# Rotary quadrants by ScalarE copies, odd Fourier tiles in the unit ring, and large elementwise operations moved from GpSimd to VectorE in a two-layer diffusion trunk

## The chip, the cores and the metric

The kernel runs on one core of a Trainium2 chip. A core has a tensor engine for matrix products (PE, with the loading of weights, PEld, shown apart), a vector engine (VectorE, DVE), a scalar engine (ScalarE, ACT), GpSimd (POOL), and SyncE (SP), whose queue here issues nearly all transfers from HBM. Each engine works through its own instructions in order and waits on semaphores for the others. The metric is the device time of one execution in microseconds; less is better.

## The reference

Two streams of 256 tokens (latent and context, width 1024) go through two layers. Each layer normalises and modulates its input, projects it by `w_in`, runs three branches, gates and merges them, and ends with a SwiGLU block. In the last layer only the latent stream is carried on. What matters here is the rotation of the queries and keys of the attention branch (latent tokens only), and the Fourier branch:

```python
def _rope(x, cos, sin):
    x1, x2 = jnp.split(x, 2, axis=-1)
    return jnp.concatenate([x1 * c - x2 * s, x1 * s + x2 * c], axis=-1)

def _fourier(u):
    z = u.astype(jnp.float32).reshape(B, T, FN_GROUPS, FN_GC)      # 4 groups of 256 channels
    y = jnp.fft.fftn(z, axes=(1, 3), norm='ortho').real
    return y.reshape(B, T, FN_W).astype(u.dtype)
```

The attention's head halves are 32 wide, so that in a layout with channels on the 128 partitions the two halves `x1` and `x2` of a head lie in neighbouring quadrants of 32 partitions. The modulation that opens a layer (a product of the conditioning vector with `w_ada`) has to be known before the first projection.

## The kernel before

**Precision.** Products of full precision are made from parts: a weight tile is loaded as float32 (`raw`), ACT rounds it to a high part (`split_hi`, L215), and the difference is the low part (`split`, L223 on POOL where `pool` is set, L225 on DVE elsewhere). Activations are held as a high and a low part too. Three products high x high, high x low and low x high are accumulated (L310 to L312 in `proj_t`).

**Jobs.** `prog` is a list of jobs, each with one weight tile of 512 KB. `run_all` goes through it: before job i runs, the tiles up to i + 4 are split and the loads up to i + 8 are issued (`upto`). The raw tiles, high parts and low parts have four buffers each. All other large tiles (activations, tables, results) are units of 4 KB a partition from a ring of 32 (`upool`, `unit()`). Transfers are issued from SP in the order in which the program names them, so one that waits for a buffer holds those behind it. Between jobs the program interleaves side work in small steps (`side`, `tick`).

**The opening.** The modulation of layer 0 is computed in four quarters (`AdaPart`: products L456, copy L461, transposing products L466, then `finish`, L470 to L472 on DVE). Each quarter lets two of the eight channel blocks of the activations be modulated (`h_banks`: L569 on ACT for the high part, L572 and L578 on DVE for the low part). `opening_jobs` runs the first four projection jobs quarter by quarter (L748), in an order written out by hand for PE, DVE, ACT and POOL (`begin`, `in_order`). In `mm(i, k, which)`, `which` 0 is high x high, 1 the low part of the weights, 2 the low part of the activations. Job 0's low part is made on POOL.

**Rotation.** Each key and query tile of 128 channels is projected into one PSUM bank of 512 columns, 256 context and 256 latent. L1476 copies the context columns by ACT. `rope` rotates the latent columns: four DVE products, one for each quadrant, that read the neighbouring quadrant of the PSUM bank and the sine table (L1317), one DVE product with the cosine table (L1318), and the sum on POOL (L1319). There are 16 such tiles a layer.

**Folding and Fourier tiles.** The transform over the tokens is split into even and odd parts. `fold_h` folds the activations while the queries are projected (the sum of high and low part at L829, on DVE for even i and on POOL for odd i; folds at L836 and L837; in layer 0 a new split at L844 and L845). `proj_z` then runs eight Fourier jobs, in pairs of an even and an odd tile of the weights (`FoldZ`). Both tiles of a pair are loaded into raw buffers. The split of a Fourier job folds the pair into a unit (L861: sum for the even one, difference for the odd one), and both splits read both raw tiles. In layer 0 (`do_split`, products L884 to L886) the folded tile is split again into parts; in layer 1 it goes to float32 products (L888), and there the odd folds are on POOL.

**Gate tile.** Behind the Fourier jobs comes `GateJob`, whose weight tile is cleared by POOL (L232), filled by four small transfers (L234) and split with its low part on POOL (L223).

Of the kernel before, what the change touches and what calls it, by code (L numbers as in the profile page):

```python
# [8 lines left out]
F32 = mybir.dt.float32  # L9
# [3 lines left out]
ALU = mybir.AluOpType  # L13
# [30 lines left out]
def tile_trunk(ctx: ExitStack, tc: tile.TileContext, x, c, cx, c_ctx, w_ada, b_ada, norm_g, w_in, ml_gate_b,  # L44
# [150 lines left out]
    class Job:  # L195

        pool = first = in_units = False
# [19 lines left out]
        def split(self):  # L217
            if not self.do_split:
                return
            self.split_hi()  # L220
            raw = self.raw
            if self.pool:
                G.tensor_tensor(out=self.lo, in0=raw, in1=self.hi.bitcast(F32), op=ALU.subtract)  # L223
            else:
                V.tensor_tensor(out=self.lo, in0=raw, in1=self.hi, op=ALU.subtract)  # L225

    class GateJob(Job):
        pool = True

# [503 lines left out]
    def opening_jobs(bd, specs, parts):  # L733
# [3 lines left out]
        def run(job):  # L737
# [11 lines left out]
            def hl(i, q):  # L749
                for k in (2 * q, 2 * q + 1):  # L750
                    mm(i, k, 2)
# [18 lines left out]
            hl(0, 0)  # L770
            for which in range(3):
                for k in range(2):
                    mm(1, k, which)
# [30 lines left out]
        for i, (cls, src, _) in enumerate(specs):  # L804
            prog.append(cls(src, KB, 128, run))
            prog[-1].first = True

            prog[-1].pool = i == 0

# [5 lines left out]
    def fold_h(h, ns, res, st):  # L815
# [8 lines left out]
        for k in range(0, KB, per):  # L824
            f = unit()
            fv = f.rearrange("p a n -> p (a n)").rearrange("p (k n) -> p k n", k=per)
            for i in range(k // 2, (k + per) // 2):
                sm = unit()[:, :, n0:]
                (G if i % 2 else V).tensor_tensor(out=sm, in0=h[0][i][:, :, n0:], in1=h[1][i][:, :, n0:], op=ALU.add)  # L829
# [20 lines left out]
    class FoldZ(Job):  # L850
# [3 lines left out]
        def load(self):  # L854
            super().load()
            self.tile = self.raw

        def split(self):
            a, b = (self.mate.tile, self.tile) if self.odd else (self.tile, self.mate.tile)
            self.raw = unit().rearrange("p a (b n) -> p (a b) n", b=4)  # L860
            (G if self.odd and not self.do_split else V).tensor_tensor(out=self.raw[:, :, 1:128], in0=a[:, :, 1:128], in1=b[:, :, 127:0:-1],  # L861
                                               op=ALU.subtract if self.odd else ALU.add)
# [449 lines left out]
    def rope(ps, u):  # L1312

        r = tmp(256)
        for a in range(4):
            src = slice(32 * (a ^ 1), 32 * (a ^ 1) + 32)
            V.tensor_tensor(out=r[32 * a:32 * a + 32, :], in0=ps[src, 256:512], in1=ropes[src, :], op=ALU.mult)  # L1317
        V.tensor_tensor(out=u[:, 256:512], in0=ps[:, 256:512], in1=ropec, op=ALU.mult)  # L1318
        G.tensor_tensor(out=u[:, 256:512], in0=u[:, 256:512], in1=r, op=ALU.add)  # L1319
# [402 lines left out]
def make_consts():  # L1722
# [13 lines left out]
    k[:, C_RS:C_RS + 256] = np.tile(np.concatenate([np.sin(ang).T, -np.sin(ang).T]), (2, 1))  # L1736
# [37 lines left out]
```

## Time and profile before

| | |
|---|---|
| median of 3 runs | 1935.72 us (1934.77 to 1935.95) |
| the profiled execution's own time | 1936.41 us |
| its span in the profile | 1934.7 us |
| PE, DVE, ACT, POOL busy | 97%, 62%, 40%, 7% of the span |
| largest groups of POOL | L1319 42.0 us, L1338 23.0 us |
| mean HBM traffic | 140 GB/s over the span |

Times in the profile are microseconds from the start of the span. A row of the order of time gives start, duration, engine, line, operation, written tile `<-` read tiles, shape, and in brackets the idle time of the engine before it and what ended it. A row of a group gives the count, the total busy time in us, the mean of one in ns, and the idle time before. A row of the waits gives the total in us, how often, and the longest. PE's products overlap, so that a product's duration is longer than the distance to the next one. POOL's L1338 lies in the attention stage, behind the stages that are changed here.

### The profile page before, as it was taken

Reading aid. Unit: us, or ns where it says so; the run is one execution under the profiler, and the core shown is the slowest. Engines: PE = TensorE matmul, PEld = TensorE weight load, DVE = VectorE, ACT = ScalarE, POOL = GpSimd, SP = SyncE. Lnnn points to the kernel's source line nnn. Section 1 sums busy time; section 2 is a strip of 40 time slices with the busy share of each in tenths; the row PEclk is TensorE's granted clock in tenths of the full one; section 3 lists DMA queues with packets and bytes.
Section 4 is the critical chain, followed back from the end, with each engine's and each line's share of the span. In section 5 each row is a group of like instructions: output and inputs, shape, how many; then the busy total and the mean of one; then the engine's idle time right before and its main releaser. Section 6 shows DMA issues by size and latency. Waiting matters only on the chain. (4 is left out here: it accounts for less than half of the span.)

```text
span 1934.7 us, 27570 instructions
## 1 busy us (share of the span) xinstructions
PE 1885.0 (97%) x10428; PEld 1579.5 (82%) x10428; DVE 1201.4 (62%) x2626; ACT 782.5 (40%) x1470; POOL 144.8 (7%) x168
## 2 busy tenths in 40 slices
PE   7999999999999999999999999999999999999998
PEld 4778787888877888788777887887888889979996
DVE  5796688852467567653334235777985477666655
ACT  3333476632343333352222224323873354345442
POOL 0231100000001110000000000150100011000000
PEclk9999999999999999999999999999999999999999
DMA  9557522134322334534442333675322664676663
GB/s 311 183 163 211 177 66 66 55 91 128 109 66 71 100 99 122 194 96 138 127 141 88 120 98 110 186 204 190 99 67 77 186 194 123 180 240 178 183 197 129
DMA packets 339679, 268.99 MB, mean 139 GB/s; under 512 B 17181, under 2 KB 295933, under 8 KB 339546
## 3 DMA queue, kind: packets, MB, share of 16 engines
q1 hardware_dynamic: 338824, 264.60, 45.9%
q10 hardware_dynamic: 722, 2.62, 0.3%
q8 instruction: 82, 1.34, 0.3%
q14 instruction: 51, 0.42, 0.1%
HBM read 264.44 MB, written 6.91 MB: 140 GB/s over the span
## 5 line engine op out<-in xcount | busy, mean ns | idle before, releaser
L225 DVE TENSOR_TENSOR wl<-wr,wh 128x1024 fp32r<-128x1024 f32 x335 | 419.0, 1253 | 408.2 <-ACT wh L215 400.8
L215 ACT CAST wh<-wr 128x1024 fp32r<-128x1024 f32 x336 | 351.9, 1050 | 651.3 <-issue 234.4
L310 PE MATMUL m<-u,wh 128*128 128x512 f32 (+1 forms) x1736 | 608.0, 350 | 0.9 <-ACT wh L215 0.9
L312 PE MATMUL m<-u,wl 128*128 128x512 f32 (+1 forms) x1736 | 595.7, 343 | 2.3 <-DVE wl L225 2.3
L311 PE MATMUL m<-u,wh 128*128 128x512 f32 (+1 forms) x1736 | 594.7, 343 | 0.0
L310 PEld LDWEIGHTS m<-u,wh 128*128 128x128 f32 x1736 | 329.1, 190 | 47.9 <-issue 4.0
L312 PEld LDWEIGHTS m<-u,wl 128*128 128x128 f32 x1736 | 328.7, 189 | 42.4 <-DVE wl L225 3.6
L311 PEld LDWEIGHTS m<-u,wh 128*128 128x128 f32 x1736 | 329.2, 190 | 38.2 <-issue 3.1
L331 PE MATMUL m<-wh,u 128*128 128x512 f32 x532 | 214.9, 404 | 0.0
L333 PE MATMUL m<-wh,u 128*128 128x512 f32 x532 | 207.9, 391 | 0.0
L332 PE MATMUL m<-wl,u 128*128 128x512 f32 x532 | 207.9, 391 | 0.0
L331 PEld LDWEIGHTS m<-wh,u 128*128 128x128 f32 x532 | 100.0, 188 | 24.3 <-issue 4.5
L333 PEld LDWEIGHTS m<-wh,u 128*128 128x128 f32 x532 | 99.9, 188 | 21.0
L332 PEld LDWEIGHTS m<-wl,u 128*128 128x128 f32 x532 | 100.1, 188 | 20.5 <-issue 1.4
L1360 ACT ACTIVATE u<-p,s 128x512 f32<-128x512 f32 (+1 forms) x96 | 59.4, 618 | 39.3 <-DVE s L1359 37.2
L623 PE MATMUL m<-wh,u 128*128 128x512 f32 x180 | 70.3, 391 | 0.2 <-ACT wh L215 0.2
L624 PE MATMUL m<-wl,u 128*128 128x512 f32 x180 | 70.1, 390 | 0.0
L625 PE MATMUL m<-wh,u 128*128 128x512 f32 x180 | 69.9, 389 | 0.0
L1319 POOL TENSOR_TENSOR u<-u,t 128x256 f32<-128x256 f32 x32 | 42.0, 1312 | 304.1 <-DVE u L1318 254.5
L1626 DVE SCALAR_TENSOR_TENSOR t<-t,m 128x512 f32<-128x512 f32 (+1 forms) x44 | 24.4, 554 | 63.2 <-PE m L312 62.7
L1357 DVE TENSOR_REDUCE s<-p 128x1 f32<-128x512 f32 (+1 forms) x96 | 57.1, 595 | 6.6 <-PE p L1355 6.4
L1317 DVE TENSOR_TENSOR t<-m,ctab 32x256 f32<-32x256 f32 x120 | 50.5, 421 | 4.1 <-ACT u L1476 1.2
(308 smaller groups left out, 2518.6 us busy)
## 6 DMA issues: line engine op xcount, KB each, us to landing
wr<-in_w_in_dram SPq DMA_DIRECT2D x176, 512.0 KB
wr<-in_w_ffn_in_dram SPq DMA_DIRECT2D x88, 512.0 KB
u<-in_w_ada_dram SPq DMA_DIRECT2D x80, 512.0 KB
wr<-in_w_ffn_out_dram SPq DMA_DIRECT2D x44, 512.0 KB
u<-in_w_ada_dram SPq DMA_DIRECT2D x32, 256.0 KB
wr<-in_w_br_da_dram SPq DMA_DIRECT2D x16, 512.0 KB
wr<-in_w_br_ml_dram SPq DMA_DIRECT2D x16, 512.0 KB
wr<-in_w_out_dram SPq DMA_DIRECT2D x16, 512.0 KB
```

Of the source, the lines that this page charges most:

```text
L215: S.copy(self.hi, self.raw)
L225: V.tensor_tensor(out=self.lo, in0=raw, in1=self.hi, op=ALU.subtract)
L310: T.matmul(ps[:, n0:], lhsT=job.hi[:, k, :], rhs=ah, start=(k == 0), stop=False)
L311: T.matmul(ps[:, n0:], lhsT=job.hi[:, k, :], rhs=al, start=False, stop=False)
L312: T.matmul(ps[:, n0:], lhsT=job.lo[:, k, :], rhs=ah, start=False, stop=(k == KB - 1))
L331: T.matmul(st[tb], lhsT=ah, rhs=job.hi[:, j, :], start=(k == 0), stop=False)
L332: T.matmul(st[tb], lhsT=ah, rhs=job.lo[:, j, :], start=False, stop=False)
L333: T.matmul(st[tb], lhsT=al, rhs=job.hi[:, j, :], start=False, stop=(k == nk - 1))
L623: T.matmul(ps[tb], lhsT=ah, rhs=job.hi[:, j, :], start=(k == 0), stop=False)
L624: T.matmul(ps[tb], lhsT=ah, rhs=job.lo[:, j, :], start=False, stop=False)
L625: T.matmul(ps[tb], lhsT=al, rhs=job.hi[:, j, :], start=False, stop=(k == nk - 1))
L1360: S.activation(p[:, m, :nk], sp[:, :nk], AF.Exp, bias=nb, scale=0.125, accum_out=d[:, m:m + 1])
```

## The change

- **Opening:** job 0's low part is made on DVE, like all others. The first products of the opening are put in another order: behind job 0's products with the high part of the activations come job 1's with the high part of the weights, then both jobs' products with the low part of the activations, then job 1's with the low part of the weights.
- **Rotation:** ACT copies each quadrant of the latent columns from PSUM into its neighbour's place in an SBUF tile `r`, and DVE multiplies `r` with the sine table in one operation over 128 partitions and adds it. The sign of the sine table is exchanged, since it is now read at the place of the result.
- **Folding:** all sums of `fold_h` and all folds of `FoldZ` are on DVE.
- **Fourier tiles:** the odd tile of a pair is loaded into a unit of the ring, the even one into a raw buffer as before.
- **Gate tile:** its low part is made on DVE. POOL still clears it.

```diff
     class Job:
-        pool = first = in_units = False
+        first = in_units = False
...
             raw = self.raw
-            if self.pool:
-                G.tensor_tensor(out=self.lo, in0=raw, in1=self.hi.bitcast(F32), op=ALU.subtract)
-            else:
-                V.tensor_tensor(out=self.lo, in0=raw, in1=self.hi, op=ALU.subtract)
+            V.tensor_tensor(out=self.lo, in0=raw, in1=self.hi, op=ALU.subtract)
 
     class GateJob(Job):
-        pool = True
-
...
             h(0, 0)
-            hl(0, 0)
-            for which in range(3):
+            for i, which in ((1, 0), (0, 2), (1, 2), (1, 1)):
                 for k in range(2):
-                    mm(1, k, which)
+                    mm(i, k, which)
...
-            prog[-1].pool = i == 0
...
                 sm = unit()[:, :, n0:]
-                (G if i % 2 else V).tensor_tensor(out=sm, in0=h[0][i][:, :, n0:], in1=h[1][i][:, :, n0:], op=ALU.add)
+                V.tensor_tensor(out=sm, in0=h[0][i][:, :, n0:], in1=h[1][i][:, :, n0:], op=ALU.add)
...
         def load(self):
-            super().load()
+            if self.odd:
+
+                self.raw = unit().rearrange("p a (b n) -> p (a b) n", b=4)
+                nc.sync.dma_start(self.raw, self.src.rearrange("(k p) n -> p k n", p=128))
+            else:
+                super().load()
             self.tile = self.raw
...
-            (G if self.odd and not self.do_split else V).tensor_tensor(out=self.raw[:, :, 1:128], in0=a[:, :, 1:128], in1=b[:, :, 127:0:-1],
-                                               op=ALU.subtract if self.odd else ALU.add)
+            V.tensor_tensor(out=self.raw[:, :, 1:128], in0=a[:, :, 1:128], in1=b[:, :, 127:0:-1],
+                            op=ALU.subtract if self.odd else ALU.add)
...
         for a in range(4):
-            src = slice(32 * (a ^ 1), 32 * (a ^ 1) + 32)
-            V.tensor_tensor(out=r[32 * a:32 * a + 32, :], in0=ps[src, 256:512], in1=ropes[src, :], op=ALU.mult)
+            S.copy(r[32 * a:32 * a + 32, :], ps[32 * (a ^ 1):32 * (a ^ 1) + 32, 256:512])
         V.tensor_tensor(out=u[:, 256:512], in0=ps[:, 256:512], in1=ropec, op=ALU.mult)
-        G.tensor_tensor(out=u[:, 256:512], in0=u[:, 256:512], in1=r, op=ALU.add)
+        V.tensor_tensor(out=r, in0=r, in1=ropes, op=ALU.mult)
+        V.tensor_tensor(out=u[:, 256:512], in0=u[:, 256:512], in1=r, op=ALU.add)
...
-    k[:, C_RS:C_RS + 256] = np.tile(np.concatenate([np.sin(ang).T, -np.sin(ang).T]), (2, 1))
+    k[:, C_RS:C_RS + 256] = np.tile(np.concatenate([-np.sin(ang).T, np.sin(ang).T]), (2, 1))
```

## The prediction

> **What bounds the kernel now.** I read the page's busy times, then who waited for whom on the tensor engine (PE), then the busy times by stretch, then the order of time in three places.
>
> ```profile
> span 1934.7 us, 27570 instructions
> PE 1885.0 (97%) x10428; PEld 1579.5 (82%) x10428; DVE 1201.4 (62%) x2626; ACT 782.5 (40%) x1470; POOL 144.8 (7%) x168
> PE m L715 <- DVE u L578: 4.8, 4, 1.3
> PE m L748 <- ACT u L569: 3.5, 1, 3.5
> PE m L888 <- DVE u L861: 2.6, 1, 2.6
> PE m L886 <- DVE wl L225: 1.9, 2, 1.7
> PE p L312 <- POOL wl L223: 1.1, 1, 1.1
> ```
>
> PE is busy 97% of the span, so an engine freed elsewhere is worth only the PE waits that end with it. The change touches the opening (L748), the Fourier tiles of layer 0 (L886) and of layer 1 (L888), and the gate tile (L223). It does not touch L715. The stretches (busy us of PE, PEld, DVE, ACT and POOL, then PE's granted clock, DMA share, GB/s) show the same places:
>
> ```profile
> 18.90:22.30 3.40, 0.19 (x1) 0.20 (x2) 2.54 (x6) 1.72 (x4) 1.56 (x1) 1.00 1.10 349
> 22.30:29.10 6.80, 6.24 (x16) 3.51 (x19) 4.93 (x9) 2.19 (x3) 0.00 (x0) 0.50 1.15 317
> 137.70:152.00 14.30, 12.31 (x95) 11.41 (x94) 14.17 (x16) 7.10 (x15) 5.29 (x6) 1.00 0.36 75
> 152.00:155.40 3.40, 3.40 (x18) 3.40 (x18) 2.23 (x3) 1.47 (x2) 0.00 (x0) 0.50 0.97 168
> 1277.00:1285.20 8.20, 5.42 (x46) 5.09 (x45) 7.97 (x16) 1.17 (x8) 6.52 (x8) 1.00 0.55 134
> 1285.20:1288.60 3.40, 3.40 (x19) 3.40 (x18) 3.31 (x3) 0.37 (x2) 3.40 (x2) 0.51 1.09 289
> ```
>
> In both Fourier stretches DVE is full (14.17 of 14.30, 7.97 of 8.20) while PE idles 1.99 and 2.78 us, and behind each idle stretch PE runs 3.4 us at half clock.
>
> **Why DVE is full there: it stands still while POOL works.** In the opening, in order of time:
>
> ```profile
> 18.12 2.34 POOL L223 TENSOR_TENSOR wl<-wr,wh 128x1024 fp32r<-128x1024 f32 x1 [16.05 <-DMA wr<-in_w_in_dram]
> 18.14 0.16 DVE L470 TENSOR_TENSOR as<-p,b1col 128x2 f32<-128x2 f32 x1 [1.02 <-PE p L466]
> 18.40 2.08 DVE L472 TENSOR_TENSOR as<-as,vcol 128x2 f32<-128x2 f32 x1
> 20.58 1.94 ACT L569 ACTIVATE u<-p,as,as 128x256 fp32r<-128x256 f32 x4 [2.53 <-DVE as L472]
> 22.11 0.64 PE L748 MATMUL m<-u,wh 128*128 128x512 f32 x1 [3.51 <-ACT u L569]
> 33.47 0.15 DVE L470 TENSOR_TENSOR as<-p,b1col 128x2 f32<-128x2 f32 x1
> 33.98 1.94 ACT L569 ACTIVATE u<-p,as,as 128x256 fp32r<-128x256 f32 x4 [1.69 <-DVE as L472]
> 34.06 0.16 DVE L472 TENSOR_TENSOR as<-as,vcol 128x2 f32<-128x2 f32 x1
> ```
>
> A two-element operation, 0.16 us at 34.06, takes 2.08 at 18.40 and ends (20.48) when POOL's ends (20.46). The same shows in the groups of 60 to 137 us and of 1215 to 1300 us, as means of one in ns:
>
> ```profile
> L1319 POOL TENSOR_TENSOR u<-u,t 128x256 f32<-128x256 f32 x32 | 42.0, 1312 | 304.1 <-DVE u L1318 254.5 <-issue 41.8 <-PE p L368 6.0
> L1317 DVE TENSOR_TENSOR t<-m,ctab 32x256 f32<-32x256 f32 x56 | 23.5, 420 | 1.2 <-ACT u L1476 0.2
> L837 DVE TENSOR_TENSOR u<-u 128x254 f32<-128x254 f32 x8 | 3.3, 414 | 0.0
> L861 DVE TENSOR_TENSOR u<-wr,wr 128x1016 f32<-128x1016 f32 x4 | 7.8, 1948 | 1.3 <-DMA wr<-in_w_in_dram 1.3
> 1289.80 1.22 DVE L861 TENSOR_TENSOR u<-wr,wr 128x1016 f32<-128x1016 f32 x1 [1.27 <-DMA wr<-in_w_in_dram]
> ```
>
> L861 costs 1.22 us free and 1.95 on average beside POOL.
>
> **The change part by part.**
>
> *Opening.* From the first L470 to ACT's L569 an unheld pass takes 33.98 - 33.47 = 0.51, so ACT starts at 18.14 + 0.51 = 18.65 instead of 20.58, and PE at 22.11 - 1.93 = 20.2. DVE, done with the small operations at 18.9 (34.06 + 0.16 - 33.47 = 0.75 after 18.14), now makes job 0's low part itself. It takes 1.22 and lies under ACT's L569. What follows:
>
> ```profile
> 24.59 2.08 PE L748 MATMUL m<-u,wh 128*128 128x512 f32 x4 [0.56 <-DVE u L578]
> 26.63 1.04 ACT L215 CAST wh<-wr 128x1024 fp32r<-128x1024 f32 x1 [3.19 <-DMA wr<-in_w_in_dram]
> 27.71 1.22 DVE L225 TENSOR_TENSOR wl<-wr,wh 128x1024 fp32r<-128x1024 f32 x1 [1.71 <-ACT wh L215]
> 28.30 2.31 PE L456 MATMUL p<-u,s 128*32 128x512 f32 x16
> 32.41 0.95 PE L466 MATMUL p<-cst,ar 128*128 128x2 f32 x8
> 37.57 1.92 PE L456 MATMUL p<-u,s 128*32 128x512 f32 x16
> ```
>
> The new order lets PE take job 1's high part before the products that need the activations' low part (L578), so the wait at 24.59 goes. The idle stretch in front of the half clock shrinks from 3.5 to 1.6 us, so I take full clock. PE's twelve products (0.26 each, half of 2.08 for four) then end between 20.2 + 3.1 = 23.3, if nothing else is late, and 28.30 - 1.93 = 26.4, if only the first wait goes: L456 starts 1.9 to 5.0 us earlier. Job 2 is late next. Its cast waited for its load until 26.63, which the change does not move; cast and low part end at 28.93. Three products of 0.26 behind it put L466 at 29.7 instead of 32.4: 2.7 gained. The load of the next quarter bounds it too: job 3 and that quarter are 2.6 MB behind 26.6, at 317 to 349 GB/s 7.5 to 8.3 us, hence 34.1 to 34.9 against the 37.57 at which PE uses it: at most 2.7 to 3.5. If L456 started only at 26.6 (products late, or its quarter landing just ahead of job 2), the way from L456 to L466, 32.41 - 28.30 = 4.1 and 0.4 less at full clock (1.92 for 2.31), would put L466 at 30.3, a gain of 2.1. I take **2.5**.
>
> *Rotation* (32 tiles). DVE gives up four L1317 of 0.42 and keeps L1318 (0.42). It gains two operations over 256 elements with both inputs in SBUF, nearest row L837 with 0.41: 2.1 becomes 1.26. POOL's 1.3 goes. ACT gains four copies of 32x256:
>
> ```profile
> 60.98 0.66 ACT L1476 COPY u<-m 128x256 f32<-128x256 f32 x2
> L838 ACT COPY u<-u 128x4 f32<-128x4 f32 x8 | 1.6, 198 | 14.0 <-DVE u L836 13.8
> 155.40:163.30 7.90, 7.90 (x68) 7.90 (x67) 3.29 (x3) 3.44 (x6) 2.49 (x1) 1.00 0.81 248
> ```
>
> One costs between 0.20 (a tiny copy) and 0.36; two L1476 took 0.66, so about 0.3, or 1.2 a tile. PE spends 2.8 us on the shortest tile (24 products of 256 columns at 7.90/68 = 0.116), ACT then 1.04 for the cast and 1.2, so ACT holds. Behind the copies, which wait for the tile's last product, stands the next weight cast. That cast runs three tiles ahead, which hides 1.2 us; only at the start of layer 1, where the cast comes just in time, the cover is gone:
>
> ```profile
> 1218.25 1.21 DVE L225 TENSOR_TENSOR wl<-wr,wh 128x1024 fp32r<-128x1024 f32 x1
> 1219.52 0.50 PE L312 MATMUL p<-u,wl 128*128 128x512 f32 x1 [0.96 <-DVE wl L225]
> ```
>
> There ACT's cast moves back by up to 1.2 and DVE's two rotations end 1.6 sooner: between a loss of 0.5 and a gain of 0.5, I take 0.
>
> *Folding, Fourier tiles, gate tile.* DVE gains the halves that POOL had: in all two L829 over 1024 elements and two over half of that, four L861 and two gate splits, each 1.22 us for 1024 elements by the free L861: 9 x 1.22 = 11 us, against 32 x 0.8 = 26 less for the rotation, and the standstills besides. So it has slack ahead of both Fourier stretches. In layer 0 a Fourier tile costs it 1.22 for the fold and 1.22 for the low part, 2.44 against PE's 24 x 0.116 = 2.8. What would be late next is the load. The DMA queue's own waits, 75 to 170 us:
>
> ```profile
> SPq L205 <- DVE u L861: 17.3, 3, 11.0
> 1298.76 0.50 PE L312 MATMUL p<-u,wl 128*128 128x512 f32 x1 [1.14 <-POOL wl L223]
> ```
>
> Loads stood 17.3 us behind the folding itself, since a pair holds two of four weight buffers until its second fold. With odd tiles in the ring of 32 units a pair holds one, and loads run twice as far ahead while DMA is at 75 GB/s: room enough. Layer 0: idle 1.99 plus half of 3.4 at half clock, 1.7, makes 3.7, of which I take **3.2**. Layer 1: 2.78 + 1.7 + 1.1 (L312's wait for the gate's low part, which POOL makes in 2.3 and DVE in 1.22) makes 5.6, of which I take **4.8**; the rest I leave for restarts that stay.
>
> **Sum.** 2.5 + 3.2 + 4.8 = 10.5. The profiled execution took 1936.41 with a span of 1934.70; the median of the runs is 1935.72, 1.0 over that span. A span of 1924.2 gives **1925.2 us**.
>
> **Rivals.**
>
> *The half-clock stretches stay.* They follow idle stretches of 2 to 3 us here, but three cases are few. Without 3.4 us the gain is 7.1: 1928.6. For it: they last 3.4 us or twice that, so the clock is set in steps, and chance decides what falls into one. Against: in each of the three cases an idle stretch (3.51, 1.99 and 2.78 us) stands right in front. The Trainium skill, "TensorE: Matmul & The Clock Gate", Part 1, says that the clock halves after an idle window of about 3.4 us and that windows run free; by it waits of 2 us alone would not have halved the clock, and the two stretches could remain. The trace's idle 1.99 and 2.78 speak against so strict a reading.
>
> *The loads are late next.* If the Fourier tiles' data, not DVE, end the waits, only the opening is won: 1933.2. For it: SP's queue is in order, and 1289.80 shows a fold that waited for its load. Against: 75 and 134 GB/s in the stalled stretches.
>
> *The ring is too short (slower).* The price comes from job 2's load:
>
> ```profile
> 19.52 2.29 SPq L205 DMA_DIRECT2D wr<-in_w_in_dram  x2
> ```
>
> Counted in the code around the fifth Fourier tile of layer 0: activations 8, keys 4, queries 4, folded activations 8, results 2, folded tiles 3, odd tiles 2: 31 of 32. From 33 on, an odd tile's load waits for a slot and holds every load behind it in SP's queue. A tile then lands some 7.1 us late (job 2: issued at 19.52, cast at 26.63) where PE uses one in 2.8. Three odd tiles would cost 3 x 4.3 = 12.9, with layer 0's 3.2 not won: 1935.7 - 2.5 - 4.8 + 12.9 = 1941.3.
>
> *It does nothing that counts*: the DVE standstill moves behind other work, 1935.7.
>
> **How the numbers follow.** Forecast 0.60, half clock stays 0.12, loads 0.14, ring 0.10, nothing 0.04. A measurement of this kernel tells about 0.2% (3.9 us) from no change, so faster means under 1931.9. Forecast, half clock and a good end of the loads' case make faster 0.75; same 0.14; slower 0.11. The range reaches from all waits won with some luck in the reshuffled buffers (2.7 + 3.7 + 5.6 + 0.5 = 12.5, and some 2 beyond: 1921.0) to the loads' case with a little lost (1934.0).
>
> **What would show it.** Right: L472 near 18.4 takes 0.16; L748 starts near 20.2 and L466 near 29.9; no half clock at 22 to 29; no wait over 1 us on L886 and L888; DVE under 85% in the Fourier stretches. Wrong: PE waiting there for a DMA or for ACT's casts, or SP held by the ring.

## The result, and the profile after

| | before | after |
|---|---|---|
| median of 4 runs each on one chip | 1935.84 us (1934.77 to 1937.80) | 1922.63 us (1921.20 to 1923.57) |
| ratio | | 0.9929, 95% interval 0.9917 to 0.9941 |
| profiled execution, its span | 1936.41, 1934.7 us | 1923.57, 1921.8 us |

The kernel is 13.2 us faster by the medians and 12.9 by the spans, where 10.5 were forecast. The page of the kernel after, with the span and the busy times:

```profile
span 1921.8 us, 27572 instructions
PE 1877.7 (98%) x10428; PEld 1575.6 (82%) x10428; DVE 1166.0 (61%) x2573; ACT 831.5 (43%) x1598; POOL 77.3 (4%) x125
```

POOL's time nearly halved and ACT's rose by 49.0 us. DVE lost only 35.4 of 1201.4, although its quadrant products alone (L1317) had taken 50.5. The lines of the kernel after lie three to five lower: L748 is now L743, L472 is L467, L569 is L564, L466 is L461, L225 is L222, L310 and L312 are L305 and L307, L888 is L885. The rotation is L1313 (ACT's copies) to L1316 (the sum).

Who waited for whom on PE, the kernel after (total in us, times, longest):

```profile
PE m L710 <- DVE u L573: 4.7, 4, 1.3
PE m L307 <- DVE wl L222: 2.3, 4, 0.8
PE m L1062 <- DVE u L1048: 1.8, 2, 1.0
PE m L743 <- ACT u L564: 1.6, 1, 1.6
```

The 3.5 us of L748 fell to 1.6. The waits of L886 and L888 and the gate's wait are gone. L710 is the L715 that the change doesn't touch. By stretch (busy us of PE, PEld, DVE, ACT, POOL, then granted clock, DMA share, GB/s), first the opening, then layer 0's and layer 1's Fourier tiles, last a stretch in the middle of the span:

```profile
22.30:29.10 6.80, 5.53 (x33) 2.40 (x31) 3.57 (x6) 2.01 (x3) 0.00 (x0) 1.00 1.16 318
134.20:148.50 14.30, 14.30 (x121) 14.30 (x120) 12.42 (x14) 9.53 (x20) 0.96 (x1) 1.00 0.42 97
1270.50:1278.50 8.00, 8.00 (x74) 8.00 (x73) 8.00 (x11) 4.06 (x13) 0.94 (x1) 1.00 0.87 160
649.70:650.90 1.20, 1.20 (x7) 1.02 (x7) 0.17 (x1) 0.18 (x1) 0.00 (x0) 0.99 1.02 288
650.90:654.30 3.40, 3.40 (x10) 2.62 (x10) 0.05 (x1) 0.44 (x1) 0.00 (x0) 0.50 0.14 40
```

PE idles no more in either Fourier stretch, and both run at full clock. DVE is still full in layer 1's (8.00 of 8.00), yet nothing waits for it: a full engine costs time only where it is behind. And a half-clock stretch of 3.4 us has come up at 650.9, where the kernel before had none.

**A ledger by place.** Both kernels have 10428 tensor products. I matched them in order and took, for the same product, its start after minus its start before (so order swaps within the opening blur it by a few tenths). The differences between the ends of a stretch, in us, with the times of the kernel before:

| stretch | start to 17 | 17 to 36 (opening) | 36 to 137 | 137 to 158 (Fourier, layer 0) | 158 to 640 | 640 to 662 | 662 to 1200 | 1200 to 1225 (layer 1's start) | 1225 to 1303 (Fourier and gate, layer 1) | 1303 to end | sum |
|---|---|---|---|---|---|---|---|---|---|---|---|
| after | +0.4 | -2.9 | -0.7 | -4.6 | -0.4 | +1.6 | -0.1 | +0.3 | -7.5 | +1.1 | -12.9 |

Columns "start to 17" and "640 to 662" are not the change's work. The first varies by 1.5 us between executions (from -0.4 to +1.1 in the kernels below), ahead of all that the change touches, and the second is the half clock above.

### The profile page after: what moved, and what is told of

Same layout as the page of the kernel before. It is cut to its first block, busy times and chain, and to the rows that moved or that the text cites. A ratio compares the mean times of both kernels' runs of the same rounds, so it can differ in the third digit from the quotient of the medians.

```text
span 1921.8 us, 27572 instructions
## 1 busy us (share of the span) xinstructions
PE 1877.7 (98%) x10428; PEld 1575.6 (82%) x10428; DVE 1166.0 (61%) x2573; ACT 831.5 (43%) x1598; POOL 77.3 (4%) x125
## 4 chain that ended last, share of the span: by engine, by line
PE 81%; DVE 9%; DMA 4%; ACT 4%; issue 2%; SPq 0%; DVEq 0%; ACTq 0%; POOL 0%; POOLq 0%
PE m L307 14%; PE m L305 14%; PE m L306 14%; PE m L326 6%; PE m L328 6%; PE m L327 6%; PE p L1251 2%; DVE wl L222 2%; PE p L1215 2%; PE m L620 1%; PE m L618 1%; PE m L619 1%; PE p L363 1%; PE p L1392 1%; DMA wr<-in_w_br_da_dram 1%
## 5 line engine op out<-in xcount | busy, mean ns | idle before, releaser
L222 DVE TENSOR_TENSOR wl<-wr,wh 128x1024 fp32r<-128x1024 f32 x336 | 417.9, 1246 | 409.0 <-ACT wh L215 400.4
L305 PE MATMUL m<-u,wh 128*128 128x512 f32 (+1 forms) x1736 | 608.6, 351 | 0.9 <-ACT wh L215 0.9
L307 PE MATMUL m<-u,wl 128*128 128x512 f32 (+1 forms) x1736 | 596.4, 344 | 2.3 <-DVE wl L222 2.3
L305 PEld LDWEIGHTS m<-u,wh 128*128 128x128 f32 x1736 | 329.4, 190 | 49.0 <-issue 6.5
L307 PEld LDWEIGHTS m<-u,wl 128*128 128x128 f32 x1736 | 329.0, 190 | 41.8 <-DVE wl L222 3.6
L1392 PEld LDWEIGHTS p<-n,t 128*128 128x128 f32 x320 | 42.0, 191 | 4.4 <-ACT u L1357 0.7
L1313 ACT COPY t<-m 32x256 f32<-32x256 f32 x120 | 43.6, 363 | 4.2 <-PE m L307 2.7
```

The costliest lines, as they stand in the source:

```text
L305: T.matmul(ps[:, n0:], lhsT=job.hi[:, k, :], rhs=ah, start=(k == 0), stop=False)
L307: T.matmul(ps[:, n0:], lhsT=job.lo[:, k, :], rhs=ah, start=False, stop=(k == KB - 1))
L1392: T.matmul(op[:, :128], lhsT=at[i][:, sb * 128:sb * 128 + 128], rhs=v[:, sb, j * 128:j * 128 + 128], start=(sb == 0), stop=(sb == nb - 1))
```

## The experiments

All kernels are run once with a profile, beside the kernel before on the same chip, a_swap in five rounds. A single time tells little here: on one chip the kernel before took from 1934.61 to 1942.10 us in nine runs. So I go by places: the ledger of the kernels that tell places apart, against the same trace of before (us, as above; the columns left out are in the sum):

| kernel | time, before beside it | opening | Fourier, layer 0 | 640 to 662 | layer 1's start | Fourier and gate, layer 1 | sum |
|---|---|---|---|---|---|---|---|
| b_lo: only the low part of job 0 | 1935.76, 1939.76 | -1.6 | -1.5 | 0.0 | 0.0 | +0.3 | -0.6 |
| b_order: only the opening's order | 1934.31, 1939.76 | -1.9 | -1.5 | 0.0 | 0.0 | +0.2 | -2.1 |
| b_vsum: only the rotation's sum on DVE | 1933.16, 1939.76 | -0.3 | -4.1 | 0.0 | +0.5 | -0.3 | -3.3 |
| b_copy: only the quadrants by ACT | 1929.42, 1937.19 | -0.5 | -3.2 | 0.0 | +0.6 | -5.4 | -7.0 |
| b_rope: both | 1925.60, 1939.76 | -0.7 | -4.6 | +1.6 | +0.3 | -7.1 | -10.8 |
| b_fold: only folding and gate tile on DVE | 1936.39, 1936.52 | -0.2 | -0.1 | 0.0 | 0.0 | -1.0 | 0.0 |
| b_ring: only the ring | 1934.69, 1936.52 | -0.8 | +0.1 | +1.6 | +0.1 | -2.4 | -1.7 |
| a_noring: after without the ring | 1924.70, 1936.52 | -2.7 | -4.6 | +1.6 | +0.3 | -6.7 | -11.7 |
| a_gsum: after, the sum back on POOL | 1922.91, 1937.87 | -1.9 | -4.6 | 0.0 | +0.6 | -7.5 | -13.5 |
| a_pfold: after, odd folds back on POOL | 1923.28, 1937.19 | -1.4 | -4.6 | 0.0 | +0.3 | -5.9 | -13.1 |

Two things have to be known to read it. First, how far a column moves without an edit: the five kernels whose opening is unchanged read -0.2 to -0.8 there, and behind 1303, where no edit of these kernels lies, they read from -0.3 to +2.5. Second, the half clock lies within these columns. The kernel before runs at half clock for 3.4 us in each Fourier stretch, at 152 and at 1285 us, and a kernel that doesn't gains some 1.6 us by that alone (the +1.6 at 640 to 662 is one such stretch). In layer 0 only b_fold and b_ring have it too, in layer 1 only b_lo and b_order. With that taken out, the two Fourier columns are:

| | after | b_vsum | b_copy | b_rope | b_fold | b_ring |
|---|---|---|---|---|---|---|
| layer 0 | -3.0 | -2.5 | -1.6 | -3.0 | -0.1 | +0.1 |
| layer 1, with the gate | -5.9 | +1.3 | -3.8 | -5.5 | +0.6 | -0.8 |

The theory on record was that DVE is late because it stands still beside POOL's large operations. The rivals: it is late by the amount of its own work; the loads are late; the half-clock stretches alone are the gain.

### The opening: b_lo and b_order

```diff
-            prog[-1].pool = i == 0
```

> The kernel before with one edit: job 0's low part is made on DVE, in the old order of products. Theory 'standstill' (DVE stands still while POOL works, and the gains are those standstills): L472 near 18.4 falls from 2.08 to 0.16, the first L748 starts near 20.3 instead of 22.1, and L466 of the second quarter comes at 30.0 to 30.4 instead of 32.41, since job 2's load caps it; total 2.0 to 2.5 us less. Rival 'order' (the new order of products makes the gain): L466 moves by less than 1.

```diff
-            hl(0, 0)
-            for which in range(3):
+            for i, which in ((1, 0), (0, 2), (1, 2), (1, 1)):
                 for k in range(2):
-                    mm(1, k, which)
+                    mm(i, k, which)
```

> The kernel before with one edit: the new order of the opening's products, job 0's low part still on POOL. Standstill: the first L748 stays at 22.1, only the wait of 0.6 at 24.6 goes, L466 of the second quarter at 31.6 to 32.2, gain 0.3 to 0.8. Order: L466 near 30, gain 2 or more.

The order of time in the opening of b_lo (start, duration):

```profile
18.33 0.16 DVE L472 TENSOR_TENSOR as<-as,vcol 128x2 f32<-128x2 f32 x1
22.83 1.29 PE L748 MATMUL m<-u,wh 128*128 128x512 f32 x4 [1.51 <-DVE u L578]
25.92 3.02 PE L456 MATMUL p<-u,s 128*32 128x512 f32 x16
30.74 0.95 PE L466 MATMUL p<-cst,ar 128*128 128x2 f32 x8
```

and of b_order:

```profile
18.95 2.21 DVE L472 TENSOR_TENSOR as<-as,vcol 128x2 f32<-128x2 f32 x1
24.66 2.02 PE L748 MATMUL m<-u,wh 128*128 128x512 f32 x6
31.12 0.95 PE L466 MATMUL p<-cst,ar 128*128 128x2 f32 x8
```

Without POOL's operation L472 takes 0.16 and the next stage starts 2 us sooner; but then PE waits 1.51 for L578, a half clock follows (L456 takes 3.02), and L466 comes at 30.74 instead of 32.41. With the new order alone the 2.21 stay and the wait for L578 goes, and L466 comes at 31.12, more than the 0.3 to 0.8 that I expected of it. Both together: 30.00 in the kernel after. So each edit alone brings 1.3 to 1.7 of the 2.4 us, b_lo a little less than the standstill had expected of it (2.0 to 2.5), b_order between its two theories. They don't add up: in the kernel after PE comes early enough to wait 0.6 us for job 2's low part, whose load lands no sooner, as the forecast had it. In both runs the half clock behind the opening lasted 3.4 us instead of 6.8, so a part of each gain is the clock's, and the two edits' own shares are not told apart from it.

### Copies or sum: b_vsum, b_copy, b_rope, a_gsum

The kernel before with one line changed, the sum on DVE:

```diff
-        G.tensor_tensor(out=u[:, 256:512], in0=u[:, 256:512], in1=r, op=ALU.add)
+        V.tensor_tensor(out=u[:, 256:512], in0=u[:, 256:512], in1=r, op=ALU.add)
```

> The kernel before with one edit: the rotation's sum on DVE instead of POOL, the four products by quadrants stay on DVE. DVE's own work grows by 0.42 us a tile (13 us in all), and POOL's 42 us of sums beside it go. Standstill: layer 0's Fourier waits shrink by half or more, gain 2 to 5 us in all. Rival 'work' (DVE's own work, 0.8 us a tile, is what the change took away, not the standstills): no gain or a loss of up to 3 us.

The whole rotation as in the kernel after (with the sine table's sign):

```diff
-            src = slice(32 * (a ^ 1), 32 * (a ^ 1) + 32)
-            V.tensor_tensor(out=r[32 * a:32 * a + 32, :], in0=ps[src, 256:512], in1=ropes[src, :], op=ALU.mult)
+            S.copy(r[32 * a:32 * a + 32, :], ps[32 * (a ^ 1):32 * (a ^ 1) + 32, 256:512])
...
-        G.tensor_tensor(out=u[:, 256:512], in0=u[:, 256:512], in1=r, op=ALU.add)
+        V.tensor_tensor(out=r, in0=r, in1=ropes, op=ALU.mult)
+        V.tensor_tensor(out=u[:, 256:512], in0=u[:, 256:512], in1=r, op=ALU.add)
```

> The kernel before with one edit: the rotation by ACT's copies, its sum on DVE; folds and gate stay on POOL. Standstill: nearly all of layer 0's Fourier waits go (L829 on POOL alone is left there), 3 to 4.4 of 4.4 us; of layer 1's 7.5 us the wait of 2.8 shrinks below 1.5 and the gate's wait of 1.1 stays; in all 5 to 8 us less than before. Rival 'loads' (the odd tiles in the ring make the gain): under 2 us in all.

b_copy is b_rope with its last line on POOL, `G.tensor_tensor(...)`; a_gsum is the kernel after with that line on POOL:

```diff
-        V.tensor_tensor(out=u[:, 256:512], in0=u[:, 256:512], in1=r, op=ALU.add)
+        G.tensor_tensor(out=u[:, 256:512], in0=u[:, 256:512], in1=r, op=ALU.add)
```

> The kernel before with the quadrants copied by ScalarE and multiplied in one VectorE operation, the sum left on GpSimd; folding, ring, gate and opening as before. It closes the square of copies and sum: neither 0, sum alone 3.3, both 10.8 us. VectorE's amount of work counts: a rotation takes it 2 operations of 0.42 us and a hold instead of 5 and a hold, so nearly all of the 10.8 comes, 8 to 11 us, 1925 to 1929, and the waits in the Fourier products of layer 0 (2.2 us) and in those of layer 1 (2.9 us) are gone. Standstill by GpSimd's sum counts: the sums still hold VectorE up, and 3 to 6 us come, 1931 to 1934.

> The kernel after with one line moved back: the sum that ends a rotation on GpSimd, the quadrant copies on ScalarE. The measurement by itself showed that a GpSimd operation with two operands keeps VectorE's next operation until its own end, so 30 of these sums (each about 0.6 us) can hold up VectorE some 0.4 to 0.6 us each in the stretches where it is full. Standstill counts: 3 to 8 us slower than the kernel after, 1926 to 1931, with the waits of the Fourier products of one or both layers back. Only VectorE's amount of work counts (the quadrant products taken off it are the gain, and the sum moved back takes another 0.42 us each off it): within 1 us of the kernel after, or up to 2 us faster, 1921 to 1924.

The stretches 137 to 157 and 1265 to 1287 us, columns as above, of the kernel before:

```profile
137.00:157.00 20.00, 18.01 (x130) 17.11 (x129) 17.94 (x18) 9.36 (x18) 6.88 (x7) 0.91 0.49 102
1265.00:1287.00 22.00, 19.14 (x142) 16.09 (x142) 21.48 (x42) 1.58 (x13) 14.41 (x11) 0.96 0.54 150
```

of b_vsum:

```profile
137.00:157.00 20.00, 19.71 (x164) 19.50 (x163) 17.60 (x20) 10.43 (x20) 4.32 (x3) 1.00 0.58 133
1265.00:1287.00 22.00, 18.24 (x150) 17.08 (x150) 21.40 (x40) 2.11 (x13) 7.69 (x7) 1.00 0.48 121
```

of b_copy:

```profile
137.00:157.00 20.00, 18.83 (x156) 18.62 (x156) 16.49 (x16) 12.27 (x24) 5.06 (x5) 1.00 0.57 136
1265.00:1287.00 22.00, 21.71 (x190) 21.55 (x189) 12.97 (x13) 6.66 (x27) 19.34 (x14) 1.00 0.61 129
```

In layer 1 the sum leaves DVE as full as it was (21.48 before, 21.40) and PE idle 3.76 us, although POOL is down from 14.41 to 7.69. The copies empty DVE to 12.97 and PE idles 0.29, although POOL is now the fullest of all (19.34). So in layer 1 taking work off DVE was enough, with POOL working as before. How long DVE is held can be summed too, as the time of each operation above the shortest of its shape in the same trace: from 1250 to 1288 us it is 5.7 us in the kernel before, 4.6 in b_vsum and 8.6 in b_copy. b_vsum took little of the standstill away there, and b_copy, which hardly waits, has more of it than the kernel before. A kernel with the quadrants on DVE and nothing left on POOL beside it was not run, so what the standstill alone costs in layer 1 stays open.

In layer 0 it is the other way round: b_vsum, which gives DVE more work, takes most of the wait (PE idle 1.99, then 0.29), and b_copy less than half of it (1.17). Who waited on PE in b_vsum from 130 to 160 us, where the kernel before has 1.9:

```profile
PE m L886 <- DVE wl L225: 0.3, 1, 0.3
```

What had made DVE late stands ahead of the wait, in the kernel before (order of time):

```profile
123.30 3.38 POOL L829 TENSOR_TENSOR u<-u,u 128x1024 f32<-128x1024 f32 x1
124.35 3.40 DVE L861 TENSOR_TENSOR u<-wr,wr 128x1016 f32<-128x1016 f32 x1
```

A fold that takes 1.21 us alone is held 2.2, and from 120 to 150 us the holds come to 4.4. b_vsum has none of over 0.15 there, and four sums of 0.42 in their place. So b_vsum's 3.3 us are what the standstill had expected, in size and in place (layer 0's waits shrink by half or more), where the rival by work had expected no gain. b_copy's 7.0 by the ledger (7.8 by the times) lie between what the two theories had expected, and b_rope's 10.8 are more than I had expected of the rotation alone. What b_copy lacks against b_rope is 1.4 us in layer 0 and 1.7 in layer 1. The latter is the gate tile: POOL clears it right behind a sum, at 1280.6 instead of 1277.0, so its load and its cast come later (1286.9 instead of 1282.5), and POOL's low part takes 2.36 behind that; who waited for whom on PE, b_copy from 1236 to 1310 us:

```profile
PE p L312 <- POOL wl L223: 1.6, 1, 1.6
```

a_gsum closes it: with folds and gate off POOL, the 32 sums on POOL cost nothing (ledger -4.6 and -7.5, as after; 1922.91 against 1922.63). The standstill as I had told it had expected 3 to 8 us. The busy times of a_gsum say why they don't help either:

```profile
PE 1877.6 (98%) x10428; PEld 1574.6 (82%) x10428; DVE 1163.7 (61%) x2541; ACT 831.3 (43%) x1598; POOL 107.9 (6%) x157
```

DVE has 32 operations of 0.42 us fewer than in the kernel after, 13.4 us, but is only 2.3 us less busy (1166.0 - 1163.7). The missing 11.1, or 0.35 for each sum, are for the most part DVE operations held up beside POOL's. (It is an upper bound: back to back, a sum on DVE takes 0.34 us from start to start, which leaves 0.27 for each.) A sum on POOL costs DVE nearly what the sum costs DVE itself.

### Folding, gate and ring: b_fold, a_pfold, b_ring, a_noring

The kernel before with the folds and the gate's low part on DVE:

```diff
-        pool = True
...
-                (G if i % 2 else V).tensor_tensor(out=sm, in0=h[0][i][:, :, n0:], in1=h[1][i][:, :, n0:], op=ALU.add)
+                V.tensor_tensor(out=sm, in0=h[0][i][:, :, n0:], in1=h[1][i][:, :, n0:], op=ALU.add)
...
-            (G if self.odd and not self.do_split else V).tensor_tensor(out=self.raw[:, :, 1:128], in0=a[:, :, 1:128], in1=b[:, :, 127:0:-1],
+            V.tensor_tensor(out=self.raw[:, :, 1:128], in0=a[:, :, 1:128], in1=b[:, :, 127:0:-1],
```

> The kernel before with the folding sums, the folding differences and the gate tile's low part on VectorE; rotation, ring and opening stay as before. Standstill (a large two-input GpSimd operation holds VectorE's operations up): the gate's wait of 1.1 us at the end of layer 1's Fourier products goes, and part of the 2.9 us wait ahead of it; 1 to 4 us in all, 1932 to 1935. VectorE's load (what counts is how much VectorE has to do in the stretch that is full): nothing is taken off VectorE, the folds are put on it, so no gain or a loss of up to 2 us, 1936 to 1938. After the run with the rotation alone, which brought 10.8 of 13.2 us, I hold the second for as likely as the first. Of this a half-clock stretch that comes or goes is worth 1.6 us either way.

a_pfold is the kernel after with the folding's odd sums and layer 1's odd folds back on POOL, and the gate tile left on DVE:

```diff
-                V.tensor_tensor(out=sm, in0=h[0][i][:, :, n0:], in1=h[1][i][:, :, n0:], op=ALU.add)
+                (G if i % 2 else V).tensor_tensor(out=sm, in0=h[0][i][:, :, n0:], in1=h[1][i][:, :, n0:], op=ALU.add)
...
-            V.tensor_tensor(out=self.raw[:, :, 1:128], in0=a[:, :, 1:128], in1=b[:, :, 127:0:-1],
+            (G if self.odd and not self.do_split else V).tensor_tensor(out=self.raw[:, :, 1:128], in0=a[:, :, 1:128], in1=b[:, :, 127:0:-1],
```

> The kernel after with the folding's odd sums and layer 1's odd folds back on GpSimd; nothing else differs. The folds' place does not count, since VectorE has slack once the quadrants are off it: within 1 us of the kernel after, 1921.6 to 1923.6. Standstill counts: each of the six large operations holds VectorE for 1.9 to 2.9 us in the full stretches, and 2 to 6 us are lost, 1924.6 to 1928.6, with waits of over 1 us in layer 1's Fourier products.

b_ring has only the odd tiles' load of the change; a_noring is the kernel after without it:

```diff
-            super().load()
+            if self.odd:
+
+                self.raw = unit().rearrange("p a (b n) -> p (a b) n", b=4)
+                nc.sync.dma_start(self.raw, self.src.rearrange("(k p) n -> p k n", p=128))
+            else:
+                super().load()
```

> The kernel before with the odd Fourier tiles read into the ring and nothing else. The tiles were not what the products waited for: less than 1 us either way, 1935 to 1937, the waits of 2.2 us in layer 0 and 2.9 us in layer 1 stay as they are. Loads are what is late: those waits go, 3 to 7 us faster. Ring too short: slower by 2 us or more, with waits of the ring's units for their last reader.

> The kernel after with the odd Fourier tiles read into the weight buffers again, as before. Not the tiles: within 1 us of the kernel after. Loads: the waits of layers 0 and 1 come back, 3 to 6 us slower than the kernel after, 1926 to 1929.

The folds alone bring nothing (1936.39 against 1936.52, and 0.0 by the ledger). The same stretch of b_fold:

```profile
1265.00:1287.00 22.00, 18.91 (x151) 16.27 (x144) 21.54 (x43) 1.84 (x13) 10.36 (x9) 1.00 0.44 117
```

DVE full as before, PE idle 3.09. That is what the amount of DVE's work had expected. Put back on POOL in the kernel after, they cost 1.6 us in layer 1 (-5.9 for -7.5), between the 1 of the one theory and the 2 to 6 of the other: one of DVE's folds takes 4.10 us there instead of 1.21, and PE waits 0.8 and 0.4. The total (1923.28 against 1922.63) shows less, but a_pfold has no half clock at 650 us. So POOL's operations still cost something with the quadrants off DVE, though less than the quadrants did. The ring is worth 0.8 us in the kernel after (-6.7 for -7.5 in layer 1, the same in layer 0), and 0.5 of that is PE's wait for the gate's low part, which a_noring has. By the spans a_noring is 1.2 us slower (1923.0 - 1921.8), but 0.8 of them lie ahead of 17 us, where nothing differs. The loads were not what is late next. The ring of 32 units did run out once: the DMA queue's own waits of the kernel after, 75 to 170 us, have

```profile
SPq L850 <- DVE u L829: 9.4, 1, 9.4
```

L850 is the load of an odd tile into the ring, and it stood 9.4 us, with all loads behind it, until a fold had read its unit. It cost nothing that shows: PE waits for nothing from 75 to 160 us.

b_ring alone, which I expected within 1 us, reads -2.4 in layer 1. Of that 1.6 is the half clock, which it doesn't have there, and the rest fits the gate's wait of 1.1, which is gone; the waits for the folds stay (2.7 us). The cast of the gate tile on ACT stood so (order of time) in the kernel before, in b_ring and in the kernel after, given here as the answer on the tile `wg` (duration ns min/median/max, first and last start):

```profile
L215 ACT CAST wh<-wg x1: 1046/1046/1046, 1295.2 to 1295.2; 128x1024 fp32r<-128x1024 f32 x1
```

```profile
L215 ACT CAST wh<-wg x1: 1047/1047/1047, 1290.4 to 1290.4; 128x1024 fp32r<-128x1024 f32 x1
```

```profile
L215 ACT CAST wh<-wg x1: 1048/1048/1048, 1275.1 to 1275.1; 128x1024 fp32r<-128x1024 f32 x1
```

The products with the tile's low part begin at 1298.76 before and 13.8 us sooner after, but the cast comes 20.1 us sooner. The tile takes a weight buffer that the Fourier tiles hold; freed sooner, it is cleared, loaded and cast sooner (it is cleared at 1289.1 before, 1281.1 in b_ring and 1265.4 after). In b_fold, which makes the low part on DVE in 1.2 us but has the cast at 1294.9, PE still waited 0.4 of the 1.1; in b_rope, which makes it on POOL in 2.35 but has the cast at 1282.5, PE didn't wait. So the faster low part shortens the gate's wait, and the earlier load ends it without that.

### The standstill by itself: probe

The kernel after, with this ahead of its work:

```diff
+        for kind in ("two", "one", "fill"):
+            for train in ("tt", "ts"):
+                V.memset(pa[:, 0:1], 1.0)
+                if kind == "two":
+                    G.tensor_tensor(out=pb, in0=pa, in1=pa, op=ALU.add)
+                elif kind == "one":
+                    G.tensor_copy(pb, pa)
+                else:
+                    G.tensor_copy(pb[:, 0:1], pa[:, 0:1])
+                    G.memset(pb, 0.0)
+                    G.memset(pb, 0.0)
+                for i in range(16):
+                    if train == "tt":
+                        V.tensor_tensor(out=pc[:, 2:4], in0=pc[:, 0:2], in1=pc[:, 0:2], op=ALU.add)
+                    else:
+                        V.tensor_scalar(out=pc[:, 2:4], in0=pc[:, 0:2], scalar1=2.0, scalar2=None, op0=ALU.mult)
```

> The kernel after with a measurement ahead of its work: six times a long GpSimd operation on 128x1024 (two operands, one operand, a fill; each twice) and beside it a train of 16 tiny VectorE operations on 128x2, once with two operands and once with one. It adds work and leaves none out, so its total says nothing. Shared port as an exclusive lock: beside the GpSimd operation with two operands, and beside the copy, the train of two-operand operations does not run at its spacing alone; its first ones wait until the GpSimd operation's end (microseconds), or GpSimd's operation waits for the train; the one-operand trains and the trains beside the fill run at under 0.15 us each. Slower but not held: every train goes at up to twice its spacing, and none stands still. No standstill: all six trains have the same spacing.

The order of time in probe, from several short windows (a row that joins x operations gives the time of all):

```profile
2.46 0.16 DVE L1694 TENSOR_TENSOR pc<-pc 128x2 f32<-128x2 f32 x1
2.61 1.89 POOL L1685 TENSOR_TENSOR u<-u 128x1024 f32<-128x1024 f32 x1 [0.53 <-DVE u L1683]
2.65 1.86 DVE L1694 TENSOR_TENSOR pc<-pc 128x2 f32<-128x2 f32 x1
...
7.55 2.06 DVE L1696 TENSOR_SCALAR pc<-pc 128x2 f32<-128x2 f32 x2
7.69 1.89 POOL L1685 TENSOR_TENSOR u<-u 128x1024 f32<-128x1024 f32 x1 [3.19 <-DVE u L1683]
...
12.75 1.19 DVE L1694 TENSOR_TENSOR pc<-pc 128x2 f32<-128x2 f32 x2
12.88 1.04 POOL L1687 COPY u<-u 128x1024 f32<-128x1024 f32 x1 [3.30 <-DVE u L1683]
...
21.88 1.14 DVE L1694 TENSOR_TENSOR pc<-pc 128x2 f32<-128x2 f32 x6
22.05 0.95 POOL L1690 MEMSET u<- 128x1024 f32 x1
...
25.28 1.14 DVE L1696 TENSOR_SCALAR pc<-pc 128x2 f32<-128x2 f32 x2
25.44 0.95 POOL L1690 MEMSET u<- 128x1024 f32 x1
...
28.89 0.98 DVE L1696 TENSOR_SCALAR pc<-pc 128x2 f32<-128x2 f32 x5
```

A DVE operation on two columns takes 0.16 us alone and 1.86 beside POOL's operation of 1.89: it ends when POOL's does. Beside POOL's copy it is held too (two in 1.19). Beside a fill of 0.95 us the operations with two operands run on (six in 1.14), but the one with a single SBUF operand, `tensor_scalar`, is held (two in 1.14, where five take 0.98 with POOL idle). I had expected the trains with one operand to run on. They were held in all three cases: beside POOL's operation with two operands (two in 2.06) and beside its copy (one in 1.04) too. The standstill that the forecast inferred from one row is real, and it is whole, not a slowing down.

The Trainium skill, "SBUF — State Buffer", section "Who interferes with whom", says that VectorE and GpSimd share one pair of SBUF ports as an exclusive lock: VectorE operations with two SBUF inputs contend with GpSimd operations that read SBUF, not with those that only write, and VectorE operations in a mode that uses both ports, which `tensor_scalar` can enter, contend with GpSimd whatever it does. The trace agrees in each of the cases above (the operations with two operands held 1.86 us, held 1.0 and not held, `tensor_scalar` held beside all three, 0.9 us of it beside the fill); that `tensor_scalar` ran in such a mode here is not shown by itself.

### Layer 1's start: a_swap

The kernel after with two lines exchanged in `first_jobs`, so that the next weight tile's cast stands ahead of the rotation's copies on ACT:

```diff
-                        specs[i][2](pss[i])
                         upto("split", nx + 1 + i)
+                        specs[i][2](pss[i])
```

> The kernel after with the split of the next weight tile issued ahead of the evacuation of a first job's bank, instead of behind it, wherever first jobs are run. The four rotations there put 3 to 4 ScalarE copies of 0.36 us each ahead of the cast of the next weight tile. Copies ahead of the cast are what layer 1's start lost: the waits of 0.4 and 0.6 us there go, and some of the 0.8 us near 1707 us, so 0.5 to 2 us faster than the kernel after, 1920.5 to 1922. Not the order: no change within 0.5 us; banks are late instead (the evacuations come later): 0.5 to 2 us slower.

The order of time at layer 1's start in the kernel after:

```profile
1210.60 1.05 ACT L215 CAST wh<-wr 128x1024 fp32r<-128x1024 f32 x1
1211.70 0.50 PE L305 MATMUL p<-u,wh 128*128 128x512 f32 x1 [0.38 <-ACT wh L215]
1212.06 1.49 ACT L1313 COPY t<-m 32x256 f32<-32x256 f32 x4
1213.01 0.50 PE L307 MATMUL p<-u,wl 128*128 128x512 f32 x1 [0.58 <-DVE wl L222]
```

and in a_swap, 3 us earlier on the clock:

```profile
1206.00 1.05 ACT L215 CAST wh<-wr 128x1024 fp32r<-128x1024 f32 x1
1207.46 1.49 ACT L1313 COPY t<-m 32x256 f32<-32x256 f32 x4
1208.45 0.40 PE L305 MATMUL p<-u,wh 128*128 128x512 f32 x1
```

The cast is now done 1.4 us ahead of its use (1208.45 - 1207.05) and both waits are gone. a_swap takes 1918.28 us (1916.77 to 1919.47, five runs); to the kernel before on its chip, 1937.87, that is 0.9902 (interval 0.9884 to 0.9919), where the kernel after has 0.9929. It has the lowest median of all, but it was not run beside the kernel after, and the two intervals just overlap. Its ledger against the kernel after at layer 1's start is -1.5 us, with smaller steps of 0.4 and 1.0 where other first jobs end (836 and 1735 us), at which the kernel after waits for a low part and a_swap doesn't. Those are some 3 us, where I had expected at most 2. By the spans it is 6.8 (1921.8 - 1915.0), but that sets a_swap's fastest run against the kernel after's slowest: the half-clock stretches at 650.9 (gone) and near 1717 (3.4 instead of 6.8 us) are some 2.9 of it and the start 0.8.

## Why the prediction was right, and where it was not

**The total** was forecast at 1925.2 and measured at 1922.63, inside the range. The places were right; of the terms two were too small, and the reason given for two of them was too narrow. That the total came so near is in part luck: the three places bring 15.0 us by the ledger, not 10.5, and 2.1 net were lost elsewhere, 1.6 of them to a half clock at 650.9 that a_gsum, a_pfold and a_swap don't have.

- *Opening, 2.5:* right in its steps. By the ledger 2.9 from 17 to 36 us. The order of time of the kernel after, against the rows that the forecast named:

```profile
18.77 0.16 DVE L467 TENSOR_TENSOR as<-as,vcol 128x2 f32<-128x2 f32 x1
20.56 0.50 PE L743 MATMUL m<-u,wh 128*128 128x512 f32 x1 [1.59 <-ACT u L564]
26.83 1.05 ACT L215 CAST wh<-wr 128x1024 fp32r<-128x1024 f32 x1 [4.94 <-DMA wr<-in_w_in_dram]
29.20 0.50 PE L743 MATMUL m<-u,wl 128*128 128x512 f32 x1 [0.61 <-DVE wl L222]
30.00 0.95 PE L461 MATMUL p<-cst,ar 128*128 128x2 f32 x8
```

  0.16 for 2.08; PE starts at 20.56 (forecast 20.2); job 2's cast waits for its load until 26.83 (26.63); the next quarter's L461 comes at 30.00 (29.7, "2.7 gained"; it is 2.4). The bound by job 2's load held. The full clock there is luck: a_gsum waited the same 1.59 us at the same place and then ran at half clock from 21.5 to 28.3, gaining 1.9, and a_pfold, with the same opening and a half clock as long, gained 1.4.
- *Layer 0, "of which I take 3.2":* mis-sized, 4.6, the same in the kernel after, in b_rope and in the four kernels made from the one after. The 3.7 us were idle time by busy shares, where PE's products look longer than their distance (0.28 recorded, 0.116 apart): each restart hides part of its wait. By the distances of starts the waits alone are 2.8.
- *Layer 1, "of which I take 4.8":* mis-sized, 7.5. Besides the same undercount there were 1.0 us more ahead of the stretch that I read, near 1266.
- *"It stands still while POOL works"* as the reason that DVE is full: the step that was too narrow. The standstill is there, 1.86 us for 0.16, and it counts in the opening and in layer 0, where b_vsum, which only moved the sum, has 2.5 of the 3.0 us that are not the clock's. But it isn't what fills DVE in the stretches that the forecast read: from 137.7 to 152 us only 1.1 of DVE's 14.17 us are holds, and of the three groups of DVE that it showed for this only L861 is longer than free. In layer 1 the four quadrant products of each rotation carry it, 1.7 us of DVE that went to ACT (1.3 net, since one product over 128 partitions takes their place): there b_copy alone has 3.8 of the 5.9 us that are not the clock's, and b_vsum and b_fold lose. The forecast had the load right ("2.1 becomes 1.26") but put it second.
- *The copy, "about 0.3":* a little more. The group of the kernel after:

```profile
L1313 ACT COPY t<-m 32x256 f32<-32x256 f32 x120 | 43.6, 363 | 4.2 <-PE m L307 2.7
```

  0.36, the upper bound, 1.49 for four.
- *Layer 1's start, 0 between -0.5 and +0.5:* a loss of 0.3, from copies ahead of the cast, as the forecast said; a_swap wins it back and more.
- *The gate:* the 1.1 us went, but not only because the low part takes 1.22 instead of 2.3: by itself that left 0.4 (b_fold). The cast comes 20 us sooner, and in b_rope an earlier cast alone was enough.
- *The ring, "room enough":* its gain is under 1 us. The sign named for its being too short, SP held by the ring, did come (9.4 us), but not the price: the loads ran far enough ahead that PE never waited for it.
- *"DVE under 85% in the Fourier stretches"* was a bad sign to look for: it is 87% and 100% there, with no PE idle.
- *The rivals.* "The half-clock stretches stay" did not come true at its two places, but the forecast's reading, that they follow idle stretches of 2 to 3 us, is too strict. In b_lo and b_order layer 0's wait stood with no half clock behind it (-1.5 in the ledger is that alone). Of the kernels in which PE waited 1.2 us or more at a time for the Fourier products, three of six have the half clock behind it in layer 0 (before, b_fold, b_ring) and three of six in layer 1 (before, b_lo, b_order); where no such wait is left, none has. And in the kernel after one came at 650.9 behind some 2 us of products over one and four columns (from 647.57 on), where PE shows no idle time by its busy share; b_ring, b_rope and a_noring have it there too, the kernel before has not. The Trainium skill, "TensorE: Matmul & The Clock Gate", Part 1, says that the clock is judged over windows of about 3.4 us that run free of the program; the traces agree in that all these stretches last 3.4 or 6.8 us and come and go with the program unchanged there. The idle window of that length, which the forecast took from the same page, does not stand ahead of 650.9. So 1.6 us of each Fourier term is a draw: gained in both layers here, and lost once at 650.9.
- *Not foreseen:* 0.7 us between 36 and 137, and a loss of 1.1 behind 1303, in which L1062 waits 1.8 for a fold where the kernel before waited 1.1. The second is within what that column does in kernels with no edit there (-0.3 to +2.5). What caused these two was not tried.

## What to carry to other kernels

When an engine is full in front of a wait, sum its own work and its holds separately, from well ahead of the wait, before blaming its neighbour. In layer 0 the holds were the larger part of what could go, in layer 1 its own work: four quadrant-wise products, each as long as one over all partitions, were 1.7 us a tile that a half idle ScalarE could take. An elementwise operation with two operands moved to GpSimd gives VectorE little back, as long as VectorE works beside it on SBUF operands: here it took 0.27 of VectorE's time for 0.34 saved, by the distances of starts. And whoever moves evacuations to the engine that also prepares the next weights should put the preparation first in its queue: two exchanged lines brought 1.5 us at layer 1's start and some 3 in all.

## What the runs showed of the hardware

- A `tensor_scalar` of float32 in SBUF on VectorE is held by a GpSimd add (two in 2.06 us), a copy (one in 1.04) and a fill too (two in 1.14), while a `tensor_tensor` beside the same fill runs at its pace (0.16 each): it isn't the number of operands alone that decides who is held.
- A PSUM copy by ScalarE over 32 partitions and 256 columns takes 0.36 us, as over 128 partitions (0.37 for L1473): four quadrants cost four times one.
